# Running most of TensorE's program as a loop of two steps, with the rotation out of place and the transposed k at one fixed place

## The chip, the cores and the metric

The kernel runs on one core of one Trainium2 chip. A core has five engines that run their own instruction streams: TensorE (PE; its weight loads are shown apart as PEld), VectorE (DVE), ScalarE (ACT), GpSimd (POOL) and SyncE (SP), and 16 DMA engines that move data between the chip's memory (DRAM here) and the core's buffers: SBUF, and PSUM for TensorE's results. The metric is the device time of one execution in microseconds (us), lower is better. A profiled execution has a span, from its first to its last instruction, and its own time, which is a little longer than the span.

## What is computed

Rotary position embedding of q and k, and then all scores of every head, without a scale and without a softmax:

```
batch, seq, heads, dim = 16, 512, 16, 64          # float32 throughout
q1, q2 = q[..., :32], q[..., 32:]
q_rot = concat([q1 * cos - q2 * sin, q1 * sin + q2 * cos])     # k likewise
scores = einsum('bshd,bthd->bsht', q_rot, k_rot)  # 16 x 512 x 16 x 512
```

The inputs q and k are 33.5 MB each, the output is 268 MB. Nothing of the output can be left out, so the DMA traffic is mostly stores.

## The kernel before

**Tiling.** The 512 positions of a batch lie on 128 partitions with 4 positions each (C = 4), so that partition p holds positions 4p to 4p+3. One "step" i makes the scores of 128 positions against all 512 for all 16 heads: step i belongs to batch i // 4 and takes position i % 4 of each partition; there are 64 steps (NST). Batch 0 is worked off by groups of four heads instead, so that the work can begin when a part of q and k has come.

**One step.** Heads are taken in pairs (HP = 8 pairs). `scores(i, p)` (lines 194 to 217) does two matmuls of 64 x 128 by 64 x 512 into a PSUM tile `ps` of 128 x 1024 (three of them rotate), ScalarE copies it into the stage tile `st` (line 212), and after the eighth pair SP issues the store of the whole stage, 4 MB (line 192). Three stage tiles rotate, so a step's first copy waits until the store of three steps ago has landed.

**Rotation.** `rope(which, n)` (lines 128 to 160) is three VectorE operations on 128 x 1024 elements: the products with the signed sine go to one scratch tile `part` (line 153), the input tile is multiplied by the cosine in place (line 154), and `part`, with the halves of each head swapped, is added to it in place (line 158). So the rotated q or k stands where the raw one was loaded.

**Transposes.** TensorE needs q and k with the head's 64 elements on partitions. `transposed` (lines 165 to 189) does four TensorE transposes (line 174) of 128 x 128 each into a PSUM tile `bank` (two rotate) and copies the bank to SBUF (line 189): q into `qT` (two tiles, one step each), k into `kT` (two tiles, one batch each, 128 x 8 x 512). In step i the next step's q goes through after pairs 1 and 3 (copied by VectorE), and one quarter of the next batch's k after pairs 5 and 6 (copied by ScalarE); the rotation of q for step i+2 and of k for step i+5 stands in VectorE's order beside them (lines 269 to 291).

**Loads.** A batch's q and k are one 2 MB load each into two rotating input tiles each (lines 117 to 126), placed at the end of the third and fourth step of a batch, and issued by SP behind that step's store. SP's queue is in order: a load stands behind the store that is written ahead of it. [...]

**What sets the order.** The order of each engine's instructions is the order in which the code is written out (`manual_schedule`); all 64 steps are unrolled on all engines. A tile framework places the semaphores and the waits.

Of the kernel before, what the change touches and what calls it, by code (L numbers as in the profile page):

```python
# [7 lines left out]

@with_exitstack  # L10
def kernel(
# [19 lines left out]
    G = H // C  # L31

    const_pool = ctx.enter_context(tc.tile_pool(name="const", bufs=1))
    in_pool = ctx.enter_context(tc.tile_pool(name="in", bufs=2))
    part_pool = ctx.enter_context(tc.tile_pool(name="part", bufs=1))
    kt_pool = ctx.enter_context(tc.tile_pool(name="kt", bufs=2))
    qt_pool = ctx.enter_context(tc.tile_pool(name="qt", bufs=2))
    stage_pool = ctx.enter_context(tc.tile_pool(name="stage", bufs=3))
    ps_s_pool = ctx.enter_context(tc.psum_pool(name="ps_s", bufs=3))
    ps_t_pool = ctx.enter_context(tc.psum_pool(name="ps_t", bufs=2))  # L40

# [11 lines left out]
    ss_v = ss_t.rearrange("p c x j -> p c (x j)")  # L53

    st_first = [stage_pool.tile([P, H, S], fp32, tag="stage", name="st") for _ in range(2)]
    early = stage_pool.tile([P, 2 * C * H * D], fp32, tag="stage", name="early")
    units = {}
    used = [0]  # L60

    def load_units(which, head, heads, queues):
        n = C * heads * D
        t = early[:, used[0] : used[0] + n].rearrange("p (c e) -> p c e", c=C)
        used[0] += n
        src = dram[which][0, :, :, head : head + heads, :]
        dst = t.rearrange("p c (h d) -> p c h d", d=D)
        m = C // len(queues)
        for x, queue in enumerate(queues):
            queue.dma_start(dst[:, m * x : m * (x + 1)], src[:, m * x : m * (x + 1)])  # L70
        for h in range(0, heads, G):
            units[which, (head + h) // G] = t[:, :, D * h : D * (h + G)]

    batches = {}
# [4 lines left out]
    scratch = const_pool.tile([P, 96], fp32, name="scratch")  # L79
    tiny = [0]  # L80

    def move_cursor(n):

        y = tiny[0]
        tiny[0] += 1
        src = bass.AP(q.tensor, 512 * y, [(512, n), (64, 2), (1, 2)])
        nc.gpsimd.dma_start(scratch[:n, 4 * y : 4 * y + 4].rearrange("p (a b) -> p a b", a=2), src)

    def load_around(which, b, t):

        n, E, SMALL = 120, C * H * D, C * H * D // 8
        x = RELIEVED[which, b]
        d = dram[which][b]

        def pieces(queue, lo, hi, F):
            k = E // F
            src = bass.AP(d.tensor, d.offset + lo * E + E - F, [(E, hi - lo), (-F, k), (1, F)])
            v = t[lo:hi].rearrange("p c e -> p (c e)")  # L100
            dst = bass.AP(v.tensor, v.offset + E - F, [v.ap[0], (-F, k), (1, F)])
            queue.dma_start(dst, src)  # L102

        if x == 0:
            nc.gpsimd.inc_swdge_sem([], [], mode="reset_dge_cursor")
        else:

            move_cursor(16 - SLOW)
        if x % 2:
            move_cursor(8)  # L110
            pieces(nc.gpsimd, n, P, SMALL)
        move_cursor(SLOW + 1)
        pieces(nc.gpsimd, 0, n, E // 2)
        if not x % 2:
            pieces(nc.scalar, n, P, SMALL)

    def load(which, b):

        if b >= B:
            return  # L120
        t = in_pool.tile([P, C, H * D], fp32, tag=which + "_in", name=which + "_sb")
        batches[which, b] = t
        if (which, b) in RELIEVED:
            load_around(which, b, t)
        else:
            nc.sync.dma_start(t.rearrange("p c (h d) -> p c h d", h=H), dram[which][b])

    def rope(which, n):

        part = part_pool.tile([P, H * D], fp32, tag="part", name="part")
        if n < C:
            x = units[which, n]
# [6 lines left out]
            adds = [(x5[:, :, :, y], p5[:, :, :, 1 - y]) for y in range(2)]  # L140
        else:
            x = batches[which, n // C][:, n % C]
            sv, k1, k2 = "p (g j) -> p g j", {"j": HD}, {"j": D}
            cs = cos_t[:, n % C].unsqueeze(1).to_broadcast((P, 2 * H, HD))
            ss = ss_v[:, n % C].unsqueeze(1).to_broadcast((P, H, D))
            pv = part.rearrange(sv, **k2)
            x4 = x.rearrange("p (h x j) -> p h x j", x=2, j=HD)
            swapped = bass.AP(part.tensor, part.offset + HD, [part.ap[0], (D, H), (-HD, 2), (1, HD)])
            adds = [(x4, swapped)]
        xs, xc = x.rearrange(sv, **k2), x.rearrange(sv, **k1)  # L150

        def products():
            nc.vector.tensor_tensor(pv, xs, ss, op=mult)  # L153
            nc.vector.tensor_tensor(xc, xc, cs, op=mult)  # L154

        def sums():
            for y, z in adds:
                nc.vector.tensor_tensor(y, y, z, op=add)  # L158

        return [products, sums]  # L160

    kT = {}
    qT = {}

    def transposed(which, n, g, copy):

        bank = ps_t_pool.tile([P, 4, P], fp32, tag="ps_t", name="bank")
        for x in range(4):
            if n < C:  # L170
                src = units[which, n][:, x, P * g : P * (g + 1)]
            else:
                src = batches[which, n // C][:, n % C, P * (4 * g + x) : P * (4 * g + x + 1)]
            nc.tensor.transpose(bank[:, x, :], src, ident)  # L174
        src = bank
        if which == "q":
            if n not in qT:
                qT[n] = qt_pool.tile([P, HP, P], fp32, tag="qT", name="qT_t")
            dst = qT[n][:, 4 * g : 4 * g + 4, :]
        else:  # L180
            b = n // C
            if b not in kT:
                kT[b] = kt_pool.tile([P, HP, S], fp32, tag="kT", name="kT_t")
            if n < C:
                dst = kT[b][:, 2 * n + g].rearrange("p (t c) -> p t c", c=C)
                src = bank.rearrange("p c t -> p t c")
            else:
                dst = kT[b][:, 4 * g : 4 * g + 4, P * (n % C) : P * (n % C + 1)]
        copy(out=dst, in_=src)  # L189

    def store(i, st):
        nc.sync.dma_start(o_v[i // C, i % C], st)

    def scores(i, p, st):

        ps = ps_s_pool.tile([P, 2, S], fp32, tag="ps_s", name="ps")
        b = i // C
        if b == 0:
            c, hp = divmod(p, 2)
            lhs, rhs = qT[i][:, C * hp + c], kT[0][:, 2 * i + hp]  # L200
        else:
            lhs, rhs = qT[i][:, p], kT[b][:, p]
        for r in range(2):
            po, rh = ps[:, r, :], rhs[64 * r : 64 * r + 64, :]
            nc.tensor.matmul(  # L205
                out=po, lhsT=lhs[64 * r : 64 * r + 64, :], rhs=rh, start=True, stop=True
            )
        so, si = st[:, 2 * p : 2 * p + 2, :], ps
# [3 lines left out]
        nc.scalar.copy(out=so, in_=si)  # L212
        if b == 0 and p % 2 == 1:
            c = p // 2
            nc.sync.dma_start(o_v[0, c, :, G * i : G * (i + 1)], st[:, G * c : G * (c + 1)])
        elif b > 0 and p == HP - 1:
            store(i, st)

    def tr_act(which, n):
        for g in range(2):  # L220
            transposed(which, n, g, nc.scalar.copy)

    def run(ops):
        for op in ops:
            op()

    with tc.manual_schedule():
        nc.scalar.dma_start(sin_t, sin.rearrange("(p c) j -> p c j", c=C))
        load_units("k", 0, G, (nc.sync, nc.scalar))
        nc.sync.dma_start(cos_t, cos.rearrange("(p c) j -> p c j", c=C))  # L230
        load_units("q", 0, G, (nc.sync, nc.scalar))
        load_units("k", G, H - G, (nc.sync,))
        load_units("q", G, H - G, (nc.sync,))
        load("k", 1)
        load("q", 1)
        make_identity(nc, ident)
        nc.scalar.copy(out=ss_t[:, :, 0, :], in_=sin_t)
        nc.scalar.mul(ss_t[:, :, 1, :], sin_t, -1.0)
        for which in ("k", "q"):
            run(rope(which, 0))  # L240
            tr_act(which, 0)

        for i in range(C):
            st = st_first[i] if i < 2 else stage_pool.tile([P, H, S], fp32, tag="stage", name="st")
            if i < C - 1:
                dve = rope("k", i + 1) + rope("q", i + 1) + rope("k", C + i)
                nxt = [("k", i + 1), ("q", i + 1)]
            else:
                dve = rope("q", C) + rope("k", C + i) + rope("q", C + 1) + rope("k", 2 * C)  # L250
                nxt = [("q", C), ("k", C + i)]
            for p in range(HP):
                scores(i, p, st)
                if p in (0, 1) and i > 0:
                    run(dve[:1])
                    dve = dve[1:]
                    transposed("k", C + i - 1, p, nc.vector.tensor_copy)
                if p == 3 and i < 2:
                    load("kq"[i], 2)
                if p in (2, 6):  # L260
# [65 lines left out]
```

## Time and profile before

| what | value |
|---|---|
| three runs, median (lowest to highest) | 792.25 us (791.65 to 792.26) |
| the profiled execution, its own time | 791.71 us |
| its span | 789.9 us, so 1.8 us lie around it |
| bytes moved by DMA | 336.18 MB, of which 268.44 MB written to DRAM |
| instruction fetches on DMA queue 8 | 24 packets, 0.39 MB |
| matmul records and weight load records | 3072 and 3072 |

The first lines of the page of a profile give each engine's busy time and its share of the span. A strip of 40 digits shows the busy tenths in 40 equal slices of the span. "L212" is line 212 of the kernel. In the table of groups, the two numbers behind the bar are the busy time in all and the mean duration of one in ns; then comes the idle time of the engine just ahead of them and what ended most of it. SPq, POOLq and ACTq stand for DMAs issued by that engine. The trace also holds a record of each DMA packet (start, duration, size, queue), and of each of the 16 increments with which the parts of a DMA report that they have landed.

### The profile page before, as it was taken

The numbers are of one execution on the slowest core, as the hardware profiler recorded it, in microseconds if no ns is written. First come the engines' busy times: TensorE is split into PE (matmuls) and PEld (weight loads), VectorE is DVE, ScalarE is ACT, GpSimd is POOL, SyncE is SP. The second block draws the span as 40 slices with busy tenths as digits, with TensorE's granted clock in tenths as the row PEclk, the third lists the DMA queues.
The fourth block names the chain that finished last, engine by engine and source line by source line (L and its number), as shares of the span: only waits on it lengthen the run. The fifth ranks groups of instructions, "written<-read, shape, count | busy, mean of one in ns | idle before, by whom it ended". The sixth has DMA issues, their size and how long they took to land.

```text
span 789.9 us, 7753 instructions
## 1 busy us (share of the span) xinstructions
PE 687.7 (87%) x3072; PEld 297.4 (38%) x3072; DVE 543.8 (69%) x516; ACT 561.2 (71%) x647; POOL 11.9 (2%) x24
## 2 busy tenths in 40 slices
PE   4999998989978989798897988989899798899960
PEld 2444443433423434243343433434334343344420
DVE  7999987667855859566676666767678486587400
ACT  3888886866847868486685865877577586588770
POOL 0000000000001000000000000100000000000000
PEclk9999999999998999899899898999899899899995
DMA  9999999999999999999999999999999999999997
GB/s 353 421 426 440 429 431 435 424 434 440 428 427 429 429 425 406 428 431 436 430 431 434 427 431 427 429 432 429 427 437 422 437 433 433 428 431 436 430 431 339
DMA packets 19100, 336.18 MB, mean 426 GB/s; under 512 B 2376, under 2 KB 3656, under 8 KB 4936
## 3 DMA queue, kind: packets, MB, share of 16 engines
q1 hardware_dynamic: 16288, 324.61, 96.1%
q0 software_dynamic: 1872, 10.10, 3.1%
q10 hardware_dynamic: 904, 0.98, 0.4%
q8 instruction: 24, 0.39, 0.2%
q14 instruction: 12, 0.10, 0.0%
HBM read 67.24 MB, written 268.44 MB: 425 GB/s over the span
## 4 chain that ended last, share of the span: by engine, by line
DMA 46%; PE 39%; DVE 7%; ACT 4%; issue 1%; ACTq 0%
DMA out_dram<-st 45%; PE ps L205 29%; PE bank L174 9%; ACT st L212 4%; DVE part L153 2%; DVE early L154 1%; DVE early L158 1%; DMA early<-in_q_dram 1%; DVE k_sb L158 1%; DVE k_sb L154 1%; DVE kT_t L189 0%; DVE q_sb L154 0%; DVE q_sb L158 0%; ACTq L321 0%; DVE qT_t L189 0%
## 5 line engine op out<-in xcount | busy, mean ns | idle before, releaser
L212 ACT COPY st<-ps 128x1024 f32<-128x1024 f32 x512 | 495.0, 1020 | 193.7 <-DMA out_dram<-st 109.1
L205 PE MATMUL ps<-kT_t,qT_t 64*128 64x512 f32 x2048 | 545.6, 650 | 64.3 <-ACT st L212 64.1
L205 PEld LDWEIGHTS ps<-kT_t,qT_t 64*128 64x128 f32 x2048 | 183.3, 196 | 255.3 <-issue 135.4
L189 DVE COPY qT_t<-bank 128x512 f32<-128x512 f32 x118 | 81.5, 690 | 186.5 <-PE bank L174 186.5
L174 PEld LDWEIGHTS bank<-ident,q_sb 128*128 128x128 f32 x480 | 55.4, 151 | 100.5 <-issue 97.6
L174 PE MATMUL bank<-ident,q_sb 128*128 128x128 f32 x480 | 86.8, 308 | 0.4 <-PE ps L205 0.4
L174 PEld LDWEIGHTS bank<-ident,k_sb 128*128 128x128 f32 x480 | 50.3, 140 | 94.6 <-issue 42.3
L174 PE MATMUL bank<-ident,k_sb 128*128 128x128 f32 x480 | 78.6, 287 | 1.2 <-DVE qT_t L189 1.2
L153 DVE TENSOR_TENSOR part<-k_sb,ss_t 128x1024 f32<-128x1024 f32 x60 | 72.9, 1215 | 9.3 <-DMA k_sb<-in_k_dram 9.2
L189 ACT COPY kT_t<-bank 128x512 f32<-128x512 f32 x122 | 72.4, 598 | 6.9 <-PE bank L174 6.9
L154 DVE TENSOR_TENSOR k_sb<-k_sb,cos_t 128x1024 f32<-128x1024 f32 x60 | 73.5, 1225 | 2.0
L158 DVE TENSOR_TENSOR k_sb<-k_sb,part 128x1024 f32<-128x1024 f32 x60 | 73.5, 1225 | 2.1
L154 DVE TENSOR_TENSOR q_sb<-q_sb,cos_t 128x1024 f32<-128x1024 f32 x60 | 73.5, 1225 | 2.1
L153 DVE TENSOR_TENSOR part<-q_sb,ss_t 128x1024 f32<-128x1024 f32 x60 | 73.5, 1224 | 2.0
L158 DVE TENSOR_TENSOR q_sb<-q_sb,part 128x1024 f32<-128x1024 f32 x60 | 72.9, 1215 | 0.0
L174 PE MATMUL bank<-ident,early 128*128 128x128 f32 x64 | 10.5, 316 | 12.2 <-DVE early L158 9.7
L174 PEld LDWEIGHTS bank<-ident,early 128*128 128x128 f32 x64 | 8.3, 161 | 17.3 <-issue 13.9
L153 DVE TENSOR_TENSOR part<-early,ss_t 128x1024 f32<-128x1024 f32 x8 | 9.8, 1222 | 5.7 <-DMA early<-in_k_dram 4.9
L102 POOL DMA_DIRECT2D q_sb<-in_q_dram x3 | 2.3, 754 | 617.4 <-PE bank L174 617.4
L158 DVE TENSOR_TENSOR early<-early,part 128x512 f32<-128x512 f32 x16 | 10.3, 685 | 0.2
L154 DVE TENSOR_TENSOR early<-early,cos_t 128x1024 f32<-128x1024 f32 x8 | 9.8, 1225 | 0.3
L189 ACT COPY qT_t<-bank 128x512 f32<-128x512 f32 x10 | 5.7, 628 | 3.3 <-PE bank L174 3.3
(12 smaller groups left out, 15.9 us busy)
## 6 DMA issues: line engine op xcount, KB each, us to landing
out_dram<-st SPq DMA_DIRECT2D x60, 4096.0 KB, 25.2
k_sb<-in_k_dram SPq DMA_DIRECT2D x13, 2048.0 KB, 27.7
q_sb<-in_q_dram SPq DMA_DIRECT2D x12, 2048.0 KB, 27.6
out_dram<-st SPq DMA_DIRECT2D x16, 1024.0 KB, 14.5
q_sb<-in_q_dram POOLq DMA_DIRECT2D x3, 1920.0 KB, 29.2
k_sb<-in_k_dram POOLq DMA_DIRECT2D x2, 1920.0 KB, 43.2
early<-in_k_dram SPq DMA_DIRECT2D x1, 1536.0 KB
early<-in_q_dram SPq DMA_DIRECT2D x1, 1536.0 KB, 12.4
```

The lines of the kernel that those rows point to most:

```text
L102: queue.dma_start(dst, src)
L153: nc.vector.tensor_tensor(pv, xs, ss, op=mult)
L154: nc.vector.tensor_tensor(xc, xc, cs, op=mult)
L158: nc.vector.tensor_tensor(y, y, z, op=add)
L174: nc.tensor.transpose(bank[:, x, :], src, ident)
L189: copy(out=dst, in_=src)
L205: nc.tensor.matmul(out=po, lhsT=lhs[64 * r : 64 * r + 64, :], rhs=rh, start=True, stop=True)
L212: nc.scalar.copy(out=so, in_=si)
```

## The change

The kernel no longer uses the tile framework's waits. A small planner (`Plan`) records each operation with what it reads and writes, works out which semaphore each must wait for, and then writes the instructions out. The order of the operations on each engine is nearly that of before.

- **The loop.** Steps 6 to 59 (54 of 64) are written once on TensorE, as a loop of 27 turns of two steps. A wait in the loop compares a semaphore with a register, and the registers are increased by one at the end of each turn. The loop's first instruction is placed at the beginning of a block of 256 instructions (`head_slot`), and a turn has 64 matmuls and transposes as written (192 matmul and weight load instructions), one extra wait, one register instruction and the branch. All other engines stay unrolled.
- **Fixed places.** For every turn to name the same addresses, each tile has one place: the three `ps` tiles are taken by a list `RING` that closes after two steps; the rotated q and the rotated k have one tile each (`rot`), read by the transposes; there is one `kT`.
- **Rotation out of place.** The cosine product goes to `rot`, the sine product stays in place in the input tile, and the sum goes to `rot`: three operations of the same sizes as before. A new rotation of q (or k) must wait until the transposes have read the last one out of its `rot`, and the input tile is free as soon as the sum is done.
- **One kT.** The first three quarters of the next batch's transposed k go to `kN`, the fourth straight into `kT`. In the last step of a batch two VectorE copies (`renew`) of 128 x 4 x 384 elements bring `kN` into `kT`: one after pair 3, when TensorE has read the first half, and one after the step's last rotation, when it has read the second.
- **Order.** ScalarE's second k copy of a step stands behind the copy of pair 7, no longer ahead of it. VectorE copies both banks of q and then rotates, where before the copies stood between the parts of a rotation. TensorE's wait for a `renew` inside the loop is replaced by one for the next VectorE copy behind it, in every turn.
- **Around it.** The whole is one critical section with one more branch and one more signal from SP ahead of it and behind it. The identity is cleared by VectorE. The list `RELIEVED` and all transfers stay as they are.

The core of it:

```diff
-        part = part_pool.tile([P, H * D], fp32, tag="part", name="part")
...
-            nc.vector.tensor_tensor(pv, xs, ss, op=mult)
-            nc.vector.tensor_tensor(xc, xc, cs, op=mult)
...
-                nc.vector.tensor_tensor(y, y, z, op=add)
+        y = rot[which]
...
+            ([lambda: nc.vector.tensor_tensor(yc, xc, cs, op=mult)], ["cos"] + keys, [("rot", which)], which + "_cos"),
+            ([lambda: nc.vector.tensor_tensor(xs, xs, ss, op=mult)], ["ss"], keys, which + "_sin"),
+            ([lambda: nc.vector.tensor_tensor(y4, y4, swapped, op=add)], keys, [("rot", which)], which + "_sum"),
...
+        elif n % C < C - 1:
+            dst = kN[:, 4 * g : 4 * g + 4, P * (n % C) : P * (n % C + 1)]
...
+            dst = kT[:, 4 * g : 4 * g + 4, S - P : S]
...
+    def renew(g):
+        dst, src = kT[:, 4 * g : 4 * g + 4, : S - P], kN[:, 4 * g : 4 * g + 4, :]
+        work("DVE", [lambda: nc.vector.tensor_copy(out=dst, in_=src)], ...)
...
+    RING = [0, 1, 2, 0, 1, 2, 0, 1, 2, 0, 1, 2, 0, 1, 0, 2]
...
+    for i in range(C, NST):
+        now[0] = i
+        late = []
+        for p in range(HP):
+            scores(i, p)
+            if p == 3 and i % C == C - 1 and i + 1 < NST:
+                renew(0)
+            if p in (1, 3) and i + 1 < NST:
+                transposed("q", i + 1, p // 2, "DVE")()
+            if p == 3 and i + 2 < NST:
+                run(rope("q", i + 2))
+            if p == 5 and i + C < NST:
+                transposed("k", i + C, 0, "ACT")()
+            if p == 6 and i + C < NST:
+                late.append(transposed("k", i + C, 1, "ACT"))
+        for copy in late:
+            copy()
+        if i + 1 + C < NST:
+            run(rope("k", i + 1 + C))
+        if i % C == C - 1 and i + 1 < NST:
+            renew(1)
...
+        with nc.Fori(
+            0, TURNS, engines=OrderedEngineSet([mybir.EngineType.PE]), head_slot={mybir.EngineType.PE: 0}
+        ):
+            for o, w in loop:
+                plan.emit(nc.tensor, o, [(site, level[v]) for site, v in w.items()])
+            for v in levels:
+                nc.tensor.reg_add(level[v], level[v], 1)
```

## The prediction

> **What bounds the kernel now.** I read the page first: busy times, the strip of DMA, and the queues.
>
> ```profile
> span 789.9 us, 7753 instructions
> ...
> PE 687.7 (87%) x3072; PEld 297.4 (38%) x3072; DVE 543.8 (69%) x516; ACT 561.2 (71%) x647; POOL 11.9 (2%) x24
> ...
> DMA  9999999999999999999999999999999999999997
> ...
> q1 hardware_dynamic: 16288, 324.61, 96.1%
> q0 software_dynamic: 1872, 10.10, 3.1%
> q10 hardware_dynamic: 904, 0.98, 0.4%
> q8 instruction: 24, 0.39, 0.2%
> ```
>
> The queues' shares add to 99.8% of 16 engines' span: the DMA engines are the bound, in every slice. TensorE's 87% is not a second bound, as the chain of waits shows, read for its periods.
>
> ```profile
> 81.08 2.78 PE ps L205 x12
> ...
> 91.10 2.78 PE ps L205 x12
> ...
> 113.28 25.54 DMA out_dram<-st
> ...
> 649.81 29.32 DMA out_dram<-st
> ```
>
> Up to about 110 us a step takes 10.02 us (91.10 - 81.08): there compute sets the pace and eats into the queue of transfers. From 113 to 650 us lie eleven batches: 536.53 / 11 = 48.78 us each, 12.19 a step, with a store in the chain each time. So from there compute has 4 x 12.19 - 40.1 = 8.7 us a batch to spare. The list of waits and the row of the store instruction say how that is held:
>
> ```profile
> ACT st L212 <- DMA out_dram<-st: 109.1, 41, 6.2
> ...
> DMA to landing us min/median/max: 16.5/25.2/32.8
> ```
>
> ScalarE waits 41 times for a stage tile whose store hasn't landed. A 4 MB store takes 9.7 us by itself (eight packets of 32 KB at 1.213 us on each of 16 engines, from the packet records), so even the store that landed soonest, 16.5 us after its issue, found 6.8 us of work queued ahead of it. Delay of compute below that costs nothing.
>
> Since DMA bounds, I went to the packet records. Each engine's packets follow one another without a gap from 75 us to the end, so the last engine's load is the time. The 16 landings of the last store lie between 782.7 and 789.0 us: 6.3 us of imbalance. Two things make it. First, the 24 fetches of queue 8 (16 KB, 0.88 to 1.05 us, and the packet behind is often some 0.4 us longer), each on one engine: about 1.25 us each. Second, one engine whose 32 KB store packets take about 1.245 us instead of 1.213 while instructions run, though its loads take the usual 0.611; that is the one which the five diverted loads spare. No fetch fell on it. Followed to the end it finishes at 788.55 us, 0.06 before the very last (788.61).
>
> **The change part by part.** *Fetches.* 24 packets of 16 KB are 6,144 instructions, exactly the 3072 + 3072 records of TensorE. The new stream has ten unrolled steps of 96 and the loop once: about 5 blocks, so some 4 fetches are left and 20 go. 20 x 1.25 = 25 us of single engines, 1.6 us over 16. What the end gains is another matter: the last engine hit by fetches may lose one or two of them (1.25 to 2.5 us), but the spared, slow engine loses none, and stands 0.06 us behind. I take a gain of 0.06; the ends are 0 and 2.5.
>
> [...]
>
> *The branch.* No row has one. Lower end 0; upper end the time of a whole small transfer, 2.9 us from issue to landing (the sine table's load): a turn that had to wait for code would need about that. I take 0.3, the usual idle times that the profile calls "issue" being 0.2 to 0.8. It is TensorE's alone.
>
> *RING.* In 16 pairs, two reuse a `ps` after two pairs instead of three, so TensorE may wait for a ScalarE copy: 0 to 2 x 1.02 us a turn; I take 0.5. A turn is then 20.04 + 0.3 + 0.5 = 20.8 us against 24.39 of DMA: hidden. Both upper ends together give 20.04 + 2.9 + 2.0 = 24.9: no longer hidden.
>
> *Rotation.* Three operations of the same size as before. The new wait (rot read by the transposes) holds VectorE at the k rotation until TensorE's transposes behind pair 6; queued behind it are the q copies of the next step. In a step, copies and the q rotation end some 9.6 us after its start and those transposes about 9.2: nothing to wait for.
>
> *Renew.* Thirty copies of 128 x 1536, which no row shows. The nearest:
>
> ```profile
> L189 DVE COPY qT_t<-bank 128x512 f32<-128x512 f32 x118 | 81.5, 690 | 186.5 <-PE bank L174 186.5
> ...
> L154 DVE TENSOR_TENSOR k_sb<-k_sb,cos_t 128x1024 f32<-128x1024 f32 x60 | 73.5, 1225 | 2.0
> ...
> L158 DVE TENSOR_TENSOR early<-early,part 128x512 f32<-128x512 f32 x16 | 10.3, 685 | 0.2
> ```
>
> From 685 ns for 512 and 1225 for 1024 a line of 145 ns + 1.055 ns an element: 1.77 us. Lower end 0.69 (three times as fast as the copy out of PSUM), upper end 2.07 (three such copies). A batch's VectorE work becomes 4 x (2 x 0.69 + 6 x 1.22) + 3.5 = 38.3 of 48.8 us: hidden in the steady part, where the late copy can hold pair 4 of the next step, and ScalarE and the store behind it, by 1 to 2 us a batch.
>
> The first batch is the tight place, since VectorE is full there:
>
> ```profile
> 70.00:80.00 10.00, 9.98 (x50) 4.43 (x48) 9.86 (x10) 8.24 (x11) 0.00 (x0) 1.00 1.08 460
> ...
> 67.94 0.68 DVE L189 COPY qT_t<-bank 128x512 f32<-128x512 f32 x1
> 68.68 0.65 PE L174 MATMUL bank<-ident,k_sb 128*128 128x128 f32 x4 [1.23 <-DVE qT_t L189]
> ...
> 73.21 0.33 SPq L192 DMA_DIRECT2D out_dram<-st  x1
> ```
>
> (The windows' columns are PE, PEld, DVE, ACT and POOL busy, clock, DMA share, GB/s.) Step 3 gets the first renew ahead of the k rotation, so its transposes slip by 1.2 us and TensorE ends the step near 62; only then may the second renew run (to 63.6), then the q rotation (67.3) and the k rotation (71.0), and the q copy of step 4, which stood at 67.94, comes at 71.0. Pairs 4 to 7 and two groups of transposes follow: the first 4 MB store goes out near 77 instead of 73.2, and steps 5 and 6 keep this 3.7 us. Ahead of these stores lie 6.8 us on the last engine and, with landings 3.2 us apart there, 3.6 on the first. So the early engines run dry for 0.1 us, the late ones never: 0. With a renew at 2.07 the delay is 4.3, still 0; only with 3.1 us more than worked out is it paid.
>
> *SP, POOL, ACT queues.* SP's order is the same, so loads stay behind their stores; input tiles are free a step sooner, which only the five loads of GpSimd's queue can use, and with the engines full this moves bytes and adds none. Their meeting with the stores may shift single engines by 1 us either way; I take 0. ScalarE's late k copy lets the store go 0.6 us sooner: hidden too.
>
> *Start and end.* One more branch and signal on either side, in nobody's shadow: the nearest rows are 0.5 to 0.7 us for SP's waits on the other engines' signals. 0 to 1.4 in all; I take 0.3.
>
> **The sum**, against the profiled execution's 791.71: - 0.06 + 0.3 = 791.95, say 792.0. The median shown, 792.25, is 0.5 above that execution, so this is no change.
>
> **The rivals.** *Faster: the slow engine isn't the bound.* Its excess goes with the instructions that run (0 to 5 ns in pauses of compute, up to 60 in full work) and is absent in loads, as recording the profile would make it; then runs without a profile are set by the engines that fetches hit, and lose one to two of them, less 0.3: 791.71 - 2.0 + 0.3 = 790.0. Against it: the profiled and the other runs agree within 0.6 us. *Slower: the first batch starves the queue.* If the delay at steps 4 to 6 passes 6.8 us (a renew of over 3 us would do, or VectorE's new waits on TensorE there), each further us is paid once, since the queue is shared by all that follows: with 3 us beyond, 795. For it: VectorE is busy 9.8 of 10 us from 20 to 80 us. *Slower: a turn over 24.39 us.* It decides from 4.35 us of branch and RING together; with both upper ends, 0.55 x 27 = 15 us: 807. *The loop doesn't do what it says:* code fetched in each turn anyway, 27 or more packets for the 20 that go, some 9 us of single engines or 0.5 us over 16: 792.4, no change.
>
> **How the numbers follow.** No change, 0.48, and code fetched anyway, 0.05; faster, 0.27; starved queue, 0.14; long turn, 0.06. The likeliest is 792.0, with its own range of 791.2 to 793.4 (0 to 1.4 for the ends, 1 us for the diverted loads). To hold 8 in 10 it must take in most of the faster case, down to 789.4 (both fetches, 2.5, gained), and the starved queue's 795.0. About 0.2% (1.6 us) is what a measurement of this kernel tells from no change: faster 0.27, within 0.53, slower 0.20.
>
> **What would show it.** Queue 8 with 4 or 5 packets (24 or more: the loop's code is fetched again). The engine with 1.245 us store packets last at the end of the last store, the others some 2 us ahead of it; if they aren't, the fetches weren't what spread them. A store near 77 us as the first of 4 MB, and a shortest time to landing of 12 to 13 us; under 9.7 the queue ran dry. ScalarE still waiting for stores some 40 times; if that is gone, compute is the bound. Renew at 1.77 us. The prediction is wrong if the timed runs fall by over 1.6 us, which would make the slow engine a thing of the profile alone.

## The result and the profile after

| | before | after |
|---|---|---|
| median (lowest to highest) | 792.50 us (791.65 to 794.36) | 802.90 us (796.95 to 804.51) |
| profiled execution, its span | 791.71, 789.9 us | 803.83, 802.0 us |
| last landing of the last store, mean of its 16 landings | 789.02, 786.56 us | 798.77, 796.52 us |
| packet time beyond the usual (the excess), summed over the packets of queues 0 and 1, / 16 | 4.8 us | 13.7 us |

The changed kernel takes 1.0116 times as long (95% interval 1.0086 to 1.0146): slower, and outside the predicted 789.4 to 795.0. The last row is worked out from the packet records: what each packet took beyond the usual duration of its size (32 KB 1.213 us, 16 KB 0.611, 8 KB 0.309, and so on). The page of the changed kernel:

```profile
GB/s 340 425 427 413 418 400 430 427 437 425 442 337 433 427 431 432 431 428 438 433 427 438 430 365 434 421 432 428 435 432 424 442 433 387 429 430 433 431 433 293
...
q0 software_dynamic: 1872, 10.10, 3.4%
...
q8 instruction: 4, 0.07, 0.0%
...
L330 DVE COPY kT_t<-kN_t 128x1536 f32<-128x1536 f32 x30 | 28.7, 956 | 71.3 <-PE ps L358 71.3
```

Four fetches are left and a renew takes 0.956 us. The DMA engines are as busy as ever (their queues' shares add to 99.2% of the span, 99.8% before), but the GB/s strip has three holes that the kernel before has not: 337, 365 and 387 in slices 12, 24 and 34 of 20 us each. GpSimd's share grew from 3.1% to 3.4% with the same bytes: its packets got longer. The same three places in the windows (columns as in the prediction: busy times, clock, DMA share, GB/s), first the changed kernel, then the one before:

```profile
222.00:236.00 14.00, 9.22 (x36) 4.08 (x38) 5.61 (x6) 7.59 (x9) 0.00 (x0) 0.76 1.00 301
470.00:480.00 10.00, 7.91 (x29) 2.91 (x30) 4.95 (x6) 6.30 (x8) 0.00 (x0) 0.83 1.03 311
668.00:678.00 10.00, 7.36 (x21) 2.66 (x20) 4.21 (x5) 4.87 (x5) 0.00 (x0) 0.66 1.04 362
```

```profile
222.00:236.00 14.00, 11.37 (x48) 4.86 (x48) 7.23 (x7) 8.79 (x10) 1.89 (x3) 0.88 1.02 437
470.00:480.00 10.00, 9.97 (x40) 4.27 (x40) 6.72 (x6) 7.66 (x9) 1.88 (x3) 0.83 1.02 437
668.00:678.00 10.00, 8.74 (x40) 3.44 (x38) 8.16 (x8) 4.93 (x6) 0.63 (x1) 0.96 0.99 426
```

A DMA share of 1.00 at 301 GB/s means busy engines with slow packets: between 224 and 232 us a 16 KB packet takes 0.97 to 1.00 us in the mean and an 8 KB one 0.41 to 0.46. The POOL column tells why the two kernels differ there: before, GpSimd issues its load inside the stretch; after, it has done so already. (It is one of the five diverted loads, the list `RELIEVED` of the kernel: GpSimd issues 120 of the 128 rows, in halves of 8 KB, behind tiny transfers of its own, and the other 8 rows go in eight pieces each, by ScalarE's queue or GpSimd's.) The timeline of GpSimd, before and after:

```profile
227.75 0.76 POOL L102 DMA_DIRECT2D q_sb<-in_q_dram  x1 [225.35 <-PE bank L174]
```

```profile
217.92 0.76 POOL L167 DMA_DIRECT2D q_sb<-in_q_dram  x1 [215.25 <-DVE q_rot L277]
```

With the rotation out of place, VectorE's sum releases the input tile, not TensorE's transposes: the load goes out 10 us sooner. Before, SP's k load landed at 228.3 us, ahead of the first packet of GpSimd's q load (232.4); now the two are in transfer together from 222.6, and the k load lands at 237.1. In the chain of waits, a store in those three places takes 35 to 39 us from issue to landing, the others 22 to 30:

```profile
209.50 39.30 DMA out_dram<-st
...
458.67 36.67 DMA out_dram<-st
...
656.80 35.35 DMA out_dram<-st
```

*The sum.* The mean landing moved by 9.96 us: 8.90 of packet excess on queues 0 and 1 and 0.21 on queue 10, less 1.18 for the packets of the 20 fetches, and 2.03 that remain. Counted from the packet records, the engines stood idle 2.1 us longer (a mean over 16): 0.3 in the first 20 us, 1.2 from 76 to 100 us, and the rest between 400 and 780 us. The last landing stands 0.2 us closer to that mean, and the end behind it grew from 0.9 to 3.3 us: 9.96 - 0.2 + 2.3 = 12.1, the difference of the spans.

*Where engines ran dry.* The timeline of VectorE and then of TensorE in the changed kernel, at the turn from the first batch to the second (the bracket is the wait ahead of the instruction):

```profile
62.48 0.96 DVE L330 COPY kT_t<-kN_t 128x1536 f32<-128x1536 f32 x1 [2.87 <-PE ps L358]
...
65.86 1.22 DVE L277 TENSOR_TENSOR q_rot<-q_rot,q_sb 128x1024 f32<-128x1024 f32 x1
```

```profile
67.14 1.11 PE L299 MATMUL bank<-ident,q_rot 128*128 128x128 f32 x4 [3.00 <-DVE q_rot L277]
```

VectorE waits for TensorE at the second renew, and then TensorE waits 3.00 us for the rotation that stands behind it. The windows of the changed kernel, and SP's first 4 MB stores, show what follows:

```profile
64.00:66.00 2.00, 0.15 (x2) 0.00 (x0) 1.93 (x3) 1.87 (x3) 0.00 (x0) 1.00 1.01 426
66.00:68.00 2.00, 0.86 (x4) 0.71 (x4) 2.00 (x2) 0.00 (x0) 0.00 (x0) 0.78 1.00 422
68.00:70.00 2.00, 2.00 (x6) 0.85 (x6) 1.93 (x3) 0.00 (x0) 0.00 (x0) 0.50 1.02 430
70.00:72.00 2.00, 2.00 (x12) 0.92 (x10) 1.40 (x3) 1.64 (x2) 0.00 (x0) 0.87 1.01 426
...
78.00:80.00 2.00, 2.00 (x12) 0.84 (x12) 1.97 (x3) 2.00 (x4) 0.00 (x0) 1.00 0.69 295
...
78.20 20.37 SPq L167 DMA_DIRECT2D out_dram<-st  x3
```

From 67.12 us on the granted clock is 0.50 for 3.41 us (the trace's clock records), and the first 4 MB store goes out at 78.20 us, not 73.21. At 78 to 80 us the DMA share is 0.69: some engines have run dry. A further 1.9 us of packet excess follows at 106 to 116 us; what causes it stays open.

*The end.* The rows of GpSimd's own instructions at the kernel's closing line (least, median and greatest duration in ns), before and after:

```profile
L321 POOLq DRAIN  x3: 45/106/29456, 667.9 to 789.7; - x3
...
L321 POOLq EVENT_SEMAPHORE_RANGE_CLEAR  x1: 139/139/139, 789.5 to 789.5; - x1
```

```profile
L550 POOLq DRAIN  x3: 40/223/1529, 799.1 to 801.8; - x3
...
L550 POOLq EVENT_SEMAPHORE_RANGE_CLEAR  x1: 612/612/612, 801.1 to 801.1; - x1
```

Before, GpSimd drained its queue at 667.9 us, behind its last load and in the shadow of the stores. The critical section leaves that drain out, so it comes behind the last store and takes 1.53 us there.

### The profile page after: what moved, and what is told of

Same layout as the page of the kernel before. It is cut to its first block, busy times and chain, and to the rows that moved or that the text cites. A ratio compares the mean times of both kernels' runs of the same rounds, so it can differ in the third digit from the quotient of the medians.

```text
span 802.0 us, 7725 instructions
## 1 busy us (share of the span) xinstructions
PE 681.8 (85%) x3072; PEld 296.5 (37%) x3072; DVE 568.0 (71%) x547; ACT 561.9 (70%) x647; POOL 11.8 (1%) x23
## 4 chain that ended last, share of the span: by engine, by line
DMA 44%; PE 42%; ACT 5%; DVE 5%; issue 1%; ACTq 0%; DVEq 0%; SPq 0%
DMA out_dram<-st 44%; PE ps L358 32%; PE bank L299 10%; ACT st L370 5%; DVE st L254 1%; DVE st L251 1%; DVE q_rot L250 1%; DMA st<-in_k_dram 0%; DVE kN_t L317 0%; DVE k_sb L276 0%; DVE q_sb L276 0%; DVE q_rot L277 0%; DVE k_rot L277 0%; DVE q_rot L275 0%; DVE k_rot L275 0%
## 5 line engine op out<-in xcount | busy, mean ns | idle before, releaser
L299 PEld LDWEIGHTS bank<-ident,q_rot 128*128 128x128 f32 x480 | 55.0, 150 | 103.7 <-issue 98.0
L299 PE MATMUL bank<-ident,q_rot 128*128 128x128 f32 x480 | 86.2, 307 | 3.9 <-DVE q_rot L277 3.0
L299 PEld LDWEIGHTS bank<-ident,k_rot 128*128 128x128 f32 x480 | 50.3, 140 | 91.7 <-issue 89.2
L275 DVE TENSOR_TENSOR k_rot<-k_sb,cos_t 128x1024 f32<-128x1024 f32 x60 | 73.2, 1220 | 9.9 <-PE bank L299 9.8
L299 PE MATMUL bank<-ident,k_rot 128*128 128x128 f32 x480 | 78.5, 286 | 0.1
L276 DVE TENSOR_TENSOR q_sb<-q_sb,ss_t 128x1024 f32<-128x1024 f32 x60 | 73.5, 1226 | 2.0
L277 DVE TENSOR_TENSOR q_rot<-q_rot,q_sb 128x1024 f32<-128x1024 f32 x60 | 73.5, 1225 | 2.1
L277 DVE TENSOR_TENSOR k_rot<-k_rot,k_sb 128x1024 f32<-128x1024 f32 x60 | 73.5, 1225 | 2.1
L276 DVE TENSOR_TENSOR k_sb<-k_sb,ss_t 128x1024 f32<-128x1024 f32 x60 | 73.5, 1225 | 2.0
L275 DVE TENSOR_TENSOR q_rot<-q_sb,cos_t 128x1024 f32<-128x1024 f32 x60 | 72.9, 1215 | 0.0
L299 PEld LDWEIGHTS bank<-ident,st 128*128 128x128 f32 x64 | 8.3, 161 | 16.5 <-DVE st L254 10.8
## 6 DMA issues: line engine op xcount, KB each, us to landing
out_dram<-st SPq DMA_DIRECT2D x16, 1024.0 KB, 13.7
st<-in_q_dram SPq DMA_DIRECT2D x1, 1536.0 KB, 12.1
```

What stands on the lines that cost most here:

```text
L275: ([lambda: nc.vector.tensor_tensor(yc, xc, cs, op=mult)], ["cos"] + keys, [("rot", which)], which + "_cos"),
L276: ([lambda: nc.vector.tensor_tensor(xs, xs, ss, op=mult)], ["ss"], keys, which + "_sin"),
L277: ([lambda: nc.vector.tensor_tensor(y4, y4, swapped, op=add)], keys, [("rot", which)], which + "_sum"),
L299: fns.append(lambda x=x, src=src: nc.tensor.transpose(bank[:, x, :], src, ident))
```

## The experiments

All times are medians; ratios are to the kernel before, timed on the same chip. The excess is that of queues 0 and 1, as above. The kernel before took 792.5 to 792.7 us beside each of them.

| kernel | time, us | ratio (95% interval) | excess, us | end behind last landing, us |
|---|---|---|---|---|
| x_late | 798.09 (794.64 to 798.88) | 1.0063 (1.0046 to 1.0080) | 4.7 | 3.3 |
| x_swap | 798.34 (796.91 to 798.88) | 1.0066 (1.0053 to 1.0079) | 9.0 | 3.3 |
| x_late_swap | 795.74 (795.20 to 796.51) | 1.0037 (1.0024 to 1.0050) | 4.3 | 3.3 |
| x_drain | 801.55 (799.79 to 802.49) | 1.0104 (1.0091 to 1.0118) | 13.1 | 2.1 |
| x_end | 792.98 (792.75 to 794.25) | 1.0010 (1.0001 to 1.0019) | 4.4 | 2.1 |
| x_unrolled | 795.14 (794.15 to 795.91) | 1.0032 (1.0020 to 1.0044) | 4.6 | 3.3 |
| x_more | 795.09 (794.15 to 797.06) | 1.0038 (1.0024 to 1.0051) | 5.8 | 2.1 |
| b_overlap | 798.88 (798.56 to 799.49) | 1.0080 (1.0067 to 1.0093) | 10.8 | 0.9 |

**x_late: the early loads undone.** The transposes are recorded as readers of a key that the five diverted loads write, so these wait for TensorE again.

```diff
-        work("PE", fns, [key, "ident"], [("bank", j)], which, g)
+        raw = [("raw", which, n // C % 2, x) for x in range(2)] if n >= C else []
+        work("PE", fns, [key, "ident"] + raw, [("bank", j)], which, g)
...
-            transfer(queue, dst, src, [], [key], sem)
+            transfer(queue, dst, src, [], [key, raw[keys.index(key)]], sem)
```

> The changed kernel with one thing undone: the five loads on GpSimd's queue wait again for the last transposes that use the rotated rows (as before the change), not only for VectorE's sums. Theory 'two loads at once': in the changed kernel three of these loads start 10 us sooner, while SP's k load is in transfer, and both slow down (16 KB packets 0.95 to 1.0 us instead of 0.611, 8 KB packets 0.44 to 0.50 instead of 0.309; summed over the 16 engines 13.7 us of excess against 4.8 before). Undone, no slow stretch at 222-236, 470-480 and 668-678 us, excess back to 4 to 6 us, time 793 to 796. Rival 'the loop or the first batch costs it': the time stays at 800 or more.

The load goes out at 227.5 us and the holes are gone; windows of x_late, the last two for the first batch:

```profile
222.00:236.00 14.00, 11.68 (x50) 4.89 (x48) 8.46 (x9) 8.78 (x10) 1.89 (x3) 0.88 1.01 436
470.00:480.00 10.00, 9.79 (x40) 4.16 (x40) 6.53 (x6) 7.66 (x10) 1.88 (x3) 0.83 0.97 416
668.00:678.00 10.00, 10.00 (x42) 4.39 (x42) 7.61 (x7) 5.86 (x7) 0.75 (x1) 0.80 1.01 436
...
68.00:70.00 2.00, 2.00 (x12) 1.04 (x12) 1.97 (x4) 1.51 (x2) 0.00 (x0) 1.00 1.04 438
...
78.00:80.00 2.00, 2.00 (x12) 1.02 (x12) 1.49 (x3) 1.53 (x2) 0.00 (x0) 1.00 1.20 516
```

The excess is back at 4.7 us and the time falls by 4.8, less than expected: the timed runs lie at 794.6 to 794.9 and at 797.6 to 798.9 (those of the changed kernel at 797.0 to 797.8 and at 801.2 to 804.5). The profiled one, 794.64, has the same 3.00 us of idle TensorE as the changed kernel, yet there its clock stays at 1.00, its first 4 MB store goes out at 75.28, and no engine runs dry at 78 to 80 us. That the clock drops in the longer of them would fit, but they have no trace: argued, not shown.

**b_overlap: the meeting made in the kernel before.** No loop, no rotation out of place; three k loads of SP stand one store later.

```diff
-            elif i % C == C - 1:
+            elif i % C == C - 1 and i // C + 3 not in (6, 11, 15):
                 load("k", i // C + 3)
+            elif i % C == 0 and i // C + 2 in (6, 11, 15):
+                load("k", i // C + 2)
```

> The kernel before, with no loop, but with the k loads of batches 6, 11 and 15 placed one store later in SP's queue, so that each is in transfer while GpSimd's q load of the same batch is. Theory 'two loads at once': 16 KB packets of these three loads near 0.9 to 1.0 us, 2 to 4 us lost each time, 798 to 803 in all, with a clock and a program otherwise as before. Rival: the early loads are not to blame, the kernel before stays at 792 to 793.

It came: 16 KB packets up to 1.08 us in the mean, 6.4 us lost, and from 230 to 238 us

```profile
230.00:238.00 8.00, 8.00 (x39) 3.29 (x37) 5.51 (x6) 6.76 (x8) 0.00 (x0) 1.00 1.02 301
```

The meeting is enough by itself.

**x_swap and x_late_swap: the first batch.** One line moves.

```diff
-            renew(1)
             run(rope("q", C + 1))
+            renew(1)
```

> As x_late, and the second renew of step 3 placed behind the rotation of q for step 5. In the changed kernel VectorE waits 2.87 us for TensorE at that renew, TensorE then 3.0 us for that rotation, and the first 4 MB store goes out at 78.2 instead of 73.2. Theory 'the queue ran dry in the first batch': store of step 4 issued near 74.5, and 1 to 2 us less than x_late (792 to 794). Rival, the prediction's own view (6.8 us of queue ahead hide it): within 0.5 us of x_late.

> The changed kernel with the swap of x_late_swap alone, the early GpSimd loads kept. Theory 'two loads at once' as the main cause: the three slow stretches stay, and the time falls by 1 to 2.5 us only, 800 to 802. Rival 'the first batch's delay is what costs': 794 or less.

VectorE now rotates while TensorE finishes its pairs. Neither waits, the clock stays at 1.00, and the first 4 MB store goes out at 73.40 (x_swap) and 72.41 us (x_late_swap). Alone the swap is worth 4.6 us, more than expected: the excess at 106 to 116 us goes too (1.9), and the three meetings, which stay, cost 6.9 us of excess in its profile and not 9.1. On top of x_late it is worth 2.4, with intervals that just overlap, and all its runs (795.2 to 796.5) lie above the two shortest of x_late. So the delay was paid in the changed kernel, but the 3.00 us of waiting alone, with the clock at 1.00, were not seen to cost anything. x_late_swap stayed above the expected 794.

**x_unrolled: the loop alone.**

```diff
+        for o in pe:
+            plan.emit(nc.tensor, o, o.waits.items())
-        with nc.Fori(
...
```

> As x_late_swap, but TensorE's 54 steps written out again instead of the loop; all else (fixed tiles, rot, kN and renew, order) as there. The prediction's view 'the engines hit by fetches are not the last, so 20 fetches fewer bring next to nothing': 24 packets on queue 8 again, mean landing of the last store some 1.2 us later than in x_late_swap, but the time within 0.7 us of its 795.7. Rival 'the loop itself is a gain': 797 or more. Rival 'branch, register waits or the loop's extra signals cost': 794.5 or less.

As expected: 24 packets on queue 8, the mean landing 1.4 us later (786.88 against 785.50), and the time 0.6 us below x_late_swap, with intervals that overlap. The loop as such neither gains nor costs what could be measured.

**x_end, x_drain: the end.** One instruction is added, to x_late_swap and to the changed kernel itself.

```diff
         nc.gpsimd.wait_ge(plan.sems[("cursor",)], plan.counts[("cursor",)])
+        nc.gpsimd.drain()
```

> As x_late_swap, with GpSimd draining its queue right after its own last transfer (near 700 us) rather than behind the last store. In the changed kernel the span ends 3.3 us after the last landing, 0.9 before the change; of the 2.3 more, a GpSimd drain of 1.53 us and a clearing of semaphores of 0.61 us (0.14 before) are the longest parts. Theory 'the drain is work that only has to be done once': last landing to end of span 1.9 us, time 794.3. Rival 'the drain costs the same each time': no change from 795.7.

> The changed kernel with GpSimd's drain behind its last transfer as the only edit. Theory 'the drain is 1.5 us at the end and nothing else': 1.2 to 1.6 us less than the changed kernel (near 801.4), span ending 1.9 us behind the last landing instead of 3.3. Rival 'it does more than that' (x_end fell by 2.8 us against x_late_swap): 800.2 or less.

The row of the added line in x_drain: 28 us long, at 661.6 us, where nobody waits for it.

```profile
L510 POOLq DRAIN  x1: 27990/27990/27990, 661.6 to 661.6; - x1
```

The closing drain then takes 0.05 us, and the end shrinks from 3.3 to 2.1 us. The median of x_drain is 1.35 us lower, as expected, but that difference lies within the spread of the two kernels' runs; the 1.2 us at the end is what the profiles show. x_end gained 2.8 on x_late_swap; its last landing, 789.1 against 790.65, makes up the rest, and why that one moved is open.

**x_more: seven loads diverted instead of five.**

```diff
-    RELIEVED = {("q", 6): 0, ("k", 7): 1, ("q", 11): 2, ("k", 12): 3, ("q", 15): 4}
+    RELIEVED = {("q", 4): 0, ("k", 5): 1, ("q", 8): 2, ("k", 9): 3, ("q", 12): 4, ("k", 13): 5, ("q", 15): 6}
```

> As x_end, with seven loads on GpSimd's queue (q4, k5, q8, k9, q12, k13, q15) instead of five, all late. Theory 'the slow engine that those loads spare is the bound, once the fetches are gone': the spread of the last store's landings falls below 7.9 us and the time to 793 or less. Rival 'the five loads balance the engines already': 794 to 796, the spared engine first at the end.

A miss: 795.1, within the rival's range and 2.1 us above x_end, with the landings of the last store no closer together (6.4 us against 5.8) and 1.4 us more excess. More relief is not the missing piece.

**What in the meeting slows the packets.** These kernels are the one before with `load_around` replaced by a simpler load; each ran once and is judged by its packets, where SP's k load and the other load are in transfer together. The load is a plain one on ScalarE's queue in b_two and b_two2, and on GpSimd's in b_pool; b_two2 and b_120hw place SP's k loads two stores later, the rest one.

```diff
-            load_around(which, b, t)
+            nc.scalar.dma_start(t.rearrange("p c (h d) -> p c h d", h=H), dram[which][b])   # b_two, b_two2
+            nc.gpsimd.dma_start(t.rearrange("p c (h d) -> p c h d", h=H), dram[which][b])   # b_pool
```

> As b_overlap, but the five loads of GpSimd's queue go as plain 2 MB loads by ScalarE's hardware queue, so that three of them still meet an SP load. For the packets only; nothing spares the slow engine here, so the time will be longer anyway (805 or more). Theory 'any two loads at once slow each other': 16 KB packets of 0.85 us or more for several us near 240, 485 and 685 us. Rival 'only GpSimd's load with its half rows does it': 0.611 us there.

> As b_two, where the loads did not meet (SP's k load ended at 236 us, ScalarE's q load began at 234): the three k loads now stand two stores later, so that they are in transfer near 240-250, 490-500 and 690-700 us, within ScalarE's q loads. For the packets only. Theory 'any two loads at once slow each other': 16 KB packets of 0.85 us or more on both queues for some 10 us. Rival 'only GpSimd's load does it': 0.611 us on both.

> As b_overlap, but GpSimd's five loads in the plain form of the SP loads (128 rows, ascending, no half rows, no tiny transfers, nothing spared). For the packets only. Theory 'the pattern of half rows in descending order does it': packets of 0.611 us near 228-240 and 475-485 us. Rival 'GpSimd's queue, or any two loads at once': 0.85 us or more.

In b_two the loads missed each other, which settles nothing. In b_two2 and b_pool they met and kept 0.611 us: two loads at once are harmless. Next, two features in which the diverted loads differ, alone and together (b_both has both edits). In b_shift, one tiny transfer of GpSimd, called the shift, stands ahead of the first plain load. In b_halves each of the 128 rows goes in two halves of 8 KB, the second first. A third feature can be seen in the packet records of the kernel before: a packet starts 3 or 4 ns ahead of the end of the one before it on its engine, so engines can be followed. The 240 half rows of the diverted load that begins at 267.2 us fall on 15 engines, 15 to 17 on each, and none on the sixteenth, of whose 26 store packets in that stretch 23 took over 1.219 us.

```diff
+            nc.gpsimd.inc_swdge_sem([], [], mode="reset_dge_cursor")    # b_shift, ahead of the first plain load
+            move_cursor(SLOW + 1)
...
+            src = bass.AP(d.tensor, d.offset + F, [(2 * F, P), (-F, 2), (1, F)])    # b_halves, F = half a row
+            dst = bass.AP(v.tensor, v.offset + F, [v.ap[0], (-F, 2), (1, F)])
...
```

> [...] For the packets only. [...] Rival 'the half rows do it': 0.611 us.

> [...] For the packets only. Theory 'the half rows do it': 16 KB packets of 0.85 us or more and 8 KB packets of 0.40 us or more near 230-240 and 475-490 us. Rival 'the shift does it': 0.611 and 0.309 us.

> [...] For the packets only. Theory 'half rows and shift together': 16 KB packets of 0.85 us or more and 8 KB packets of 0.40 us or more near 230-240 us. Rival 'it takes the deal over 15 engines (120 rows)': 0.611 and 0.309 us.

None of the three slows the first meeting (438, 451 and 435 GB/s from 230 to 238 us; packets of 0.611 and 0.309 us). What was left was the number of rows: 120 by one transfer and 8 by another.

```diff
...
+            for queue, lo, hi in ((nc.gpsimd, 0, 120), (nc.scalar, 120, 128)):    # b_120w; b_120hw: nc.scalar twice
+                src = bass.AP(d.tensor, d.offset + lo * E, [(E, hi - lo), (1, E)])
+                queue.dma_start(v[lo:hi], src)
```

b_120 does the same with the 120 rows in descending halves.

> As b_halves, but only 120 rows by GpSimd (240 half rows, dealt over 15 engines, not shifted on purpose) and the last 8 rows whole by ScalarE's queue. For the packets only. Theory 'the deal over 15 engines with half rows': 16 KB packets of 0.85 us or more and 8 KB packets of 0.40 us or more near 230-240 us. Rival 'half rows and shift together': 0.611 and 0.309 us.

> As b_120, but the 120 rows of GpSimd's load are whole rows in ascending order. For the packets only. Theory 'the deal of 120 rows over 15 engines is enough': packets well over 0.611 us and some 300 to 370 GB/s near 230-238 us, where b_pool's 128 rows keep 442 GB/s. Rival 'it takes half rows as well': 0.611 us and 430 GB/s or more.

> As b_two2 (ScalarE's hardware queue instead of GpSimd's, SP's k loads two stores later), but each of the five loads as 120 and 8 rows. For the packets only. Theory 'the deal of rows, whatever queue': near 240-250 us some 300 to 370 GB/s, where b_two2 keeps 431. Rival 'only on GpSimd's queue': 430 GB/s or more, packets of 0.611 us.

Windows while the two loads meet, whole rows on GpSimd's queue, first 128 rows (b_pool), then 120 (b_120w):

```profile
230.00:238.00 8.00, 8.00 (x36) 3.40 (x36) 5.97 (x6) 6.68 (x8) 0.00 (x0) 0.92 1.03 442
```

```profile
230.00:238.00 8.00, 7.70 (x38) 3.23 (x36) 5.67 (x6) 5.76 (x8) 0.00 (x0) 1.00 1.04 305
```

And on ScalarE's hardware queue, 128 rows (b_two2), then 120 (b_120hw):

```profile
240.00:250.00 10.00, 9.04 (x44) 3.95 (x44) 0.00 (x0) 7.57 (x10) 0.00 (x0) 1.00 1.01 431
```

```profile
240.00:250.00 10.00, 7.19 (x36) 2.94 (x32) 0.00 (x0) 4.75 (x7) 0.00 (x0) 0.97 1.03 236
```

A load split into 120 and 8 rows is enough, on either queue, with whole rows or half ones (b_120: 369 GB/s from 230 to 238 us). It is the part of 120 that does it, at least on GpSimd's queue: in b_120w the packets are slow from the first of the 120 rows at 231.2 us, and the first of the eight rows starts at 238.9; in the changed kernel the slow stretch at 222 to 236 us is over before theirs start, at 239.7. The kernels with 120 rows took 816 to 826 us in all (b_120, b_120w, b_120hw), against 800 to 802 for the six others.

## Why the prediction was wrong

*The step that failed:* "input tiles are free a step sooner, which only the five loads of GpSimd's queue can use, and with the engines full this moves bytes and adds none ... I take 0". The move was seen; its price was not, since a full queue was taken for a fixed rate, and only the meeting with stores was weighed, not that with an SP load. Three of the five loads moved into the transfer of an SP load, and there the engines stay full at 301 to 362 GB/s. That is 9.1 us of packet excess in three stretches; undoing it is worth 4.8 us in timed runs, making it in the kernel before costs 6.4. The trace of before could have raised the question: GpSimd's issue at 227.75 stands beside a k load that landed at 228.3.

*First batch.* The place and the order of VectorE's work were right: the renew waits for TensorE, with both rotations behind it. The term was mis-sized in two ways. By the order of work alone the first 4 MB store went out at 75.28 (x_late, clock at 1.00), 2.1 us late and not 3.7; the clock, which the prediction did not weigh, put 2.9 more on top in the changed kernel. An estimate from the clock records gives 1.7 of it to the 3.41 us at 0.50, and 1.3 to the start: there the records grant 1.00 from 19.33 us on, before from 16.78 and in x_late from 16.61, and at 18 to 20 us TensorE did 7 matmuls, not 14. The cover was near: the store at 98.2 us landed 12.2 us after its issue, as the prediction's sign has it, more than the 9.7 that a store takes, so the last engine did not run dry. But the leading engines had 3.6 us, the delay was 5.0, and what they idle is lost: 1.2 us as a mean over the 16. "0 ... only with 3.1 us more than worked out is it paid" thus failed too; the swap that removes the delay gained 4.6 us alone and 2.4 on top of x_late. As a rival this had a chance of 0.14 and its price, 3 us, was near, but by luck: its condition, a delay over 6.8 us, was not met.

*Ends:* 0.3 taken, 1.4 at most; 2.3 at the end and 0.2 at the start measured. 1.2 of it is GpSimd's drain (the end of x_drain against that of the changed kernel), which before lay hidden at 667.9 us and which the prediction has no term for; 0.5 is the clearing of semaphores, 0.612 us instead of 0.139; the rest is not taken apart.

*What held.* Fetches: 4 packets, and no gain from the 20 that went, as x_unrolled shows (that a loop's code is not fetched again, on which the 20 rest, no row of before showed); that the slow engine is why could not be followed through the changed kernel. The branch and `RING` cost nothing: in the chain, steps 5 to 7 stand 10.01 us apart (81.93, 91.94, 101.96), and so do four late steps with turns ending among them (707.53, 717.55, 727.57, 737.58), as before (10.02). The renew at 0.956 us instead of 1.77 lies near the lower end given, and hidden in the steady part. ScalarE waits 24 times for stores, not some 40, but longer (12.3 us instead of 6.2 at most):

```profile
ACT st L370 <- DMA out_dram<-st: 94.6, 24, 12.3
```

Of the rivals, "long turn" and "code fetched anyway" are out. "Faster" isn't seen either: with all three costs undone (the meeting, the first batch, the drain), x_end is at 1.0010 (1.0001 to 1.0019) of before. No version here beats the kernel before.

## What to carry to other kernels

A buffer that comes free sooner starts its next load sooner: look up what is in transfer at that time, and take a busy DMA share together with its GB/s, since full engines moved a third less here (301 GB/s, not 437). Where VectorE and TensorE hand work to each other, put what needs nothing ahead of what waits, and count the idle time of TensorE also as clock that it may lose (here 3.00 us idle, then 0.50 for 3.41 us, in two of three profiles). A wrapper that leaves out a drain may only have moved it to the end (1.53 us here): compare the tail behind the last landing, not only the loop.

## What the hardware showed that was not expected

- Two 2 MB loads that met kept 0.611 us per 16 KB packet when both had 128 rows (b_pool, b_two2); when one had 120, both mostly took 0.8 to 1.3 us, at 236 to 369 GB/s for the core instead of 431 to 451 (b_120hw, b_120w, b_120). Alone beside stores, the 120 rows cost nothing (0.309 us per half row in the kernel before). In the kernel before, such a load's half rows fall on 15 engines (240 of them, 15 to 17 on each, at 267 us). What in this slows both loads when they meet, no run shows.
- The same 3.00 us of idle TensorE came with a granted clock of 0.50 for 3.41 us in the changed kernel and in x_drain (from 67.12 and 66.66 us), and with none in x_late. Why it came in two of the three profiles, no run shows.
- The loop of 192 matmul and weight load instructions fetched nothing turn by turn: 4 packets on queue 8 in all, at 33.8, 59.0, 89.4 and 749.5 us, where 27 turns ran; x_unrolled has 24. The 256 instructions of a block are worked out from the kernel before (6,144 records of TensorE over 24 packets); where the loop lies in a block no record shows, and no run places it elsewhere.
- Stretches of 0.6 to 1.9 us of packet excess also stand at 300 to 310 us in the kernel before, x_late and x_late_swap and at 104 to 118 us in the changed kernel and x_drain, at an SP q load beside stores, with no second load in sight. SP's k load had one too in b_shift and b_halves (16 KB packets of 0.97 and 0.95 us near 673 us), before the other load's first packet. So not every slow packet here comes from a meeting with 120 rows; the cause of these stays open.
